# Attention in a three-branch mixer: the product with the values put on token partitions, its division moved behind it, one turn back for four tiles

## The chip, the cores and the metric

The kernel runs on one core of a Trainium2 chip. The metric is the device time of one execution in microseconds (us), as the median of several runs. Five engines work side by side, each through its own list of instructions in a fixed order: PE (matrix products), DVE (vector work), ACT (activations), POOL (general work) and SP (transfers).

## The reference

Two layers, each with three sub-layers: a gated feed-forward step, a mixer, and another feed-forward step, over 512 tokens and 1024 channels in float32. The mixer adds three branches; the one that is changed is attention with a forget bias, 8 heads of 64 channels:

```python
def block(args):                      # 128 queries at a time
    qi, Fi, pi = args
    s = jnp.einsum('bhqd,bhkd->bhqk', qi, k) * scale
    s = s + (Fi[..., :, None] - F[..., None, :])
    s = jnp.where(kpos[None, :] <= pi[:, None], s, -jnp.inf)
    p = jax.nn.softmax(s, axis=-1)
    return jnp.einsum('bhqk,bhkd->bhqd', p, v)
...
o_a = _fox_attention(q, k, v, fl, f_bias) @ wpa
o_b = _rg_lru_branch(...) @ wpb
o_c = _rwkv7_branch(...) @ wpc
```

## The kernel before

Activations stay channels-on-partitions between the steps: `aout[:, p, :]` holds the 128 channels of two heads (a pair) for all 512 tokens. `mix_branches` issues three things interleaved: the attention (`fox`, four pairs per layer), then the linear recurrence (`lru`), and beside both the steps of the RWKV branch, the gate products, and background work on the next layer's conditioning vectors. The `yield` values in `fox_pair` are the costs by which the other two streams are advanced (lines 1140 to 1152). The framework's scheduler then sets every engine's order from its own estimate of durations, so an edit in the attention also moves the instructions around it. Each engine then runs its list strictly in order.

In `fox_pair`, each pair takes four query tiles `i` of 128 tokens, and for each of the two heads `hh`: two products give the scores `sc` (lines 1054, 1055); DVE adds the bias and takes the maximum (1058, and 1062 for the earlier keys); DVE negates the maximum (1066); ACT takes the exponential in place in `e` and its sum `rs` (1068); DVE inverts the sum (1069) and multiplies the whole row block by it (1070). Then PE turns `e` in 128x128 pieces (1077), ACT or DVE copies the turned block to `et` (1080, 1082), and PE multiplies with the values:

```python
mm(out=po[64 * hh : 64 * hh + 64, 0:P], lhsT=vs[:, j, hh * 64 : hh * 64 + 64],
   rhs=et[:, j * P : (j + 1) * P], start=j == 0, stop=j == i, skip_group_check=True)
```

The 64 value columns of a head are the weights and the 128 queries stream through, so the output lies channels-on-partitions, the two heads on the two halves. ACT copies it to `aout` (1091). Each such product in float32 is two instructions on PE in the trace. Per pair there are 20 products, so 160 over both layers and 320 instructions. Lines 201 to 203 are the large projections' products (512 columns), lines 194 and 196 split weights into a rounded part and a rest (the rest on POOL inside the mixer), lines 866 and 868 are an inverse of RWKV on DVE, and line 913 is an RWKV product with full weights and 64 columns.

Of the kernel before, what the change touches and what calls it, by code (L numbers as in the profile page):

```python
# [9 lines left out]
F32 = mybir.dt.float32  # L10
F32R = mybir.dt.float32r
AF = mybir.ActivationFunctionType
ALU = mybir.AluOpType
PSUM = bass.MemoryType.PSUM

P = 128
# [3 lines left out]
NT = S // P  # L20
# [9 lines left out]
DH = 64  # L30
# [29 lines left out]
class Trunk:  # L60
# [952 lines left out]
    def fox_pair(self, l, p, ap):  # L1013


        nc = self.nc
        mm = nc.tensor.matmul


        qs = ap.tile([P, 2, S], F32R, tag="q", bufs=1, name=self.nm("q"))  # L1020
        ks = ap.tile([P, 2, S], F32R, tag="k", bufs=1, name=self.nm("k"))
        kl = self.kl
        vs = ap.tile([P, NT, P], F32, tag="v", bufs=1, name=self.nm("v"))
        ps = self.gemm("aq", p)
        for hh, r in enumerate(ROWS):
            nc.scalar.activation(qs[r, hh, :], ps[r], AF.Copy)
            nc.vector.tensor_tensor(out=qs[ROWS[1 - hh], hh, :], in0=ps[r], in1=qs[r, hh, :].bitcast(F32), op=ALU.subtract)
        yield 5.2
        ps = self.gemm("ak", p)
        for hh, r in enumerate(ROWS):  # L1030
            nc.scalar.activation(ks[r, hh, :], ps[r], AF.Copy)
            nc.vector.tensor_tensor(out=kl[r, hh, :], in0=ps[r], in1=ks[r, hh, :].bitcast(F32), op=ALU.subtract)
            nc.gpsimd.tensor_copy(ks[ROWS[1 - hh], hh, :], ks[r, hh, :])
        yield 5.2
        vf = ap.tile([P, S], F32, tag="e", bufs=2, name=self.nm("vf"))
        nc.vector.tensor_copy(vf, self.gemm("av", p))
        pv = self.ps("s")
        for t in range(NT):
            nc.tensor.transpose(pv[:, t * P : (t + 1) * P], vf[:, t * P : (t + 1) * P], self.ident)
        nc.scalar.activation(vs.rearrange("p t c -> p (t c)"), pv, AF.Copy)  # L1040
        yield 5.2
        fbs = []
        for hh in range(2):
            fbs.append(ap.tile([P, S], F32, tag="fb", bufs=2, name=self.nm("fb")))
            nc.sync.dma_start(out=fbs[hh], in_=self.nF[2 * p + hh : 2 * p + hh + 1, :].broadcast_to([P, S]))
        yield 0.9
        for i in range(NT):
            n = i * P
            es = []
            for hh, fb in enumerate(fbs):  # L1050
                fm = ap.tile([P, P], F32, tag="fm", bufs=2, name=self.nm("fm"))
                nc.gpsimd.tensor_tensor(out=fm, in0=fb[:, n : n + P], in1=self.causal, op=ALU.add)
                sc = self.ps("s")
                mm(out=sc[:, 0 : n + P], lhsT=qs[:, hh, n : n + P], rhs=ks[:, hh, 0 : n + P], start=True, stop=False)
                mm(out=sc[:, 0 : n + P], lhsT=qs[:, hh, n : n + P], rhs=kl[:, hh, 0 : n + P], start=False, stop=True)
                e = ap.tile([P, S], F32, tag="e", bufs=2, name=self.nm("e"))
                m = self.sp.tile([P, 2], F32, tag="mx", name=self.nm("mx"))
                nc.vector.tensor_tensor_reduce(out=e[:, n : n + P], in0=sc[:, n : n + P], in1=fm, scale=0.125,
                                               scalar=-3e38, op0=ALU.add, op1=ALU.max, accum_out=m[:, 0:1])
                last = m[:, 0:1]  # L1060
                if i:
                    nc.vector.tensor_tensor_reduce(out=e[:, 0:n], in0=sc[:, 0:n], in1=fb[:, 0:n], scale=0.125,
                                                   scalar=last, op0=ALU.add, op1=ALU.max, accum_out=m[:, 1:2])
                    last = m[:, 1:2]
                nm = self.sp.tile([P, 1], F32, tag="nmx", name=self.nm("nmx"))
                nc.vector.tensor_scalar(out=nm, in0=last, scalar1=-1.0, scalar2=None, op0=ALU.mult)
                rs = self.sp.tile([P, 1], F32, tag="rsum", name=self.nm("rsum"))
                nc.scalar.activation(e[:, 0 : n + P], e[:, 0 : n + P], AF.Exp, bias=nm, accum_out=rs)
                nc.vector.reciprocal(rs, rs)
                nc.vector.tensor_scalar(out=e[:, 0 : n + P], in0=e[:, 0 : n + P], scalar1=rs, scalar2=None, op0=ALU.mult)  # L1070
                es.append(e)
                yield 0.2 * (i + 1)
            ets = []
            for hh, e in enumerate(es):
                pt = self.ps("s")
                for j in range(i + 1):
                    nc.tensor.transpose(pt[:, j * P : (j + 1) * P], e[:, j * P : (j + 1) * P], self.ident)
                et = ap.tile([P, S], F32, tag="et", bufs=2, name=self.nm("et"))
                if hh:
                    nc.scalar.activation(et[:, 0 : n + P], pt[:, 0 : n + P], AF.Copy)  # L1080
                else:
                    nc.vector.tensor_copy(et[:, 0 : n + P], pt[:, 0 : n + P])
                ets.append(et)
                yield 0.1 * (i + 1)

            po = self.ps("s")
            for j in range(i + 1):
                for hh, et in enumerate(ets):
                    mm(out=po[64 * hh : 64 * hh + 64, 0:P], lhsT=vs[:, j, hh * 64 : hh * 64 + 64],  # L1089
                       rhs=et[:, j * P : (j + 1) * P], start=j == 0, stop=j == i, skip_group_check=True)  # L1090
            nc.scalar.activation(self.aout[:, p, n : n + P], po[:, 0:P], AF.Copy)
            yield 0.25 * (i + 1)

    def mix_branches(self, l):

# [405 lines left out]
```

## Time and profile before

| what | value |
|---|---|
| runs | 3092.88, 3094.02, 3103.51 us; median 3094.02 |
| profiled execution | 3098.59 us, its span 3096.5 us |
| PE busy | 2931.2 us, 95% of the span |
| DVE busy | 1880.0 us, 61% |
| attention stretches | 496 to 786 us and 2028 to 2318 us of the span |
| mean granted clock of PE | 0.983 |

The busy time of PE counts overlapping products once, and its ends are modelled, so 95% means that PE is rarely without a product in flight. The numbers behind an arrow in the waits name the instruction that ended the wait. `PEld` is the load of weights, which runs beside products.

### The profile page before, as it was taken

The page shows a single profiled execution, that of the slowest core. Times are in us where ns is not written, and L with a number is a line of the kernel's source. Part 1 is how long each engine was busy: PE and PEld are TensorE (multiplying, and loading weights), DVE is VectorE, ACT ScalarE, POOL GpSimd, SP SyncE. Part 2 cuts the span into 40 slices and gives each one's busy share as a digit, 9 for nine tenths or more (in the row PEclk, how much of TensorE's full clock was granted, in tenths as well). Part 3 has the DMA queues.
Part 4 walks back from the last instruction along what each step waited for, and adds up shares of the span by engine and source line. Part 5 has one row for each costly group of instructions (what it writes and reads, how often), then busy time and mean ns, then how long its engine had stood idle before and what let it go on. Part 6 is the DMA issues. An engine that isn't in the chain of part 4 may idle for free. (4 is left out here: it accounts for less than half of the span.)

```text
span 3096.5 us, 39351 instructions
## 1 busy us (share of the span) xinstructions
PE 2931.2 (95%) x15330; PEld 2338.4 (76%) x15330; DVE 1880.0 (61%) x3534; ACT 1142.2 (37%) x1699; POOL 554.8 (18%) x379
## 2 busy tenths in 40 slices
PE   7999998998989998999999999889989899999998
PEld 5888886676766788888888887767666677788887
DVE  6755567666785656565656546667676756654435
ACT  4322253332545635222342214433335554342212
POOL 0000142333232013000130002423333320230000
PEclk9999999999999999999999999999999999999999
DMA  8634333333342463434434424433333424632221
GB/s 280 224 109 146 115 117 101 88 87 102 94 113 67 139 203 118 139 122 143 129 117 136 133 92 145 127 99 93 88 90 93 107 73 143 204 116 96 89 68 62
DMA packets 389402, 372.17 MB, mean 120 GB/s; under 512 B 54964, under 2 KB 318544, under 8 KB 389216
## 3 DMA queue, kind: packets, MB, share of 16 engines
q1 hardware_dynamic: 377048, 350.14, 37.0%
q10 hardware_dynamic: 12168, 19.53, 1.7%
q8 instruction: 120, 1.97, 0.3%
q14 instruction: 66, 0.54, 0.1%
HBM read 347.54 MB, written 22.09 MB: 119 GB/s over the span
## 5 line engine op out<-in xcount | busy, mean ns | idle before, releaser
L194 ACT ACTIVATE hi<-raw 128x1024 fp32r<-128x1024 f32 (+1 forms) x460 | 469.2, 1028 | 1248.9 <-PE pg L202 501.3
L196 POOL TENSOR_TENSOR lo<-raw,hi 128x1024 fp32r<-128x1024 f32 x164 | 408.0, 2490 | 1692.1 <-ACT hi L194 1639.2
L201 PE MATMUL pg<-hhi,hi 128*128 128x512 f32 (+1 forms) x1744 | 680.4, 393 | 13.7 <-DVE ks L645 3.7
L202 PE MATMUL pg<-hlo,hi 128*128 128x512 f32 (+1 forms) x1744 | 673.5, 389 | 2.9 <-DVE nm L343 2.9
L203 PE MATMUL pg<-hhi,lo 128*128 128x512 f32 (+1 forms) x1744 | 674.8, 391 | 0.0
L196 DVE TENSOR_TENSOR lo<-raw,hi 128x1024 fp32r<-128x1024 f32 (+1 forms) x296 | 342.5, 1165 | 301.3 <-ACT hi L194 296.1
L201 PEld LDWEIGHTS pg<-hhi,hi 128*128 128x128 f32 x1744 | 330.9, 190 | 86.9 <-issue 10.5
L203 PEld LDWEIGHTS pg<-hhi,lo 128*128 128x128 f32 x1744 | 330.6, 190 | 66.5 <-issue 2.1
L202 PEld LDWEIGHTS pg<-hlo,hi 128*128 128x128 f32 x1744 | 331.2, 190 | 65.3 <-issue 4.7
L202 PE MATMUL pr<-hlo,hi 128*128 128x512 f32 (+1 forms) x816 | 300.4, 368 | 5.1 <-DVE nm L343 2.9
L201 PE MATMUL pr<-hhi,hi 128*128 128x512 f32 (+1 forms) x816 | 301.5, 370 | 2.2 <-ACT hhi L397 2.2
L203 PE MATMUL pr<-hhi,lo 128*128 128x512 f32 (+1 forms) x816 | 300.7, 369 | 0.0
L284 DVE SCALAR_TENSOR_TENSOR acc<-raw,cact,acc 128x512 f32<-128x512 f32 x224 | 187.7, 838 | 48.7 <-DMA raw<-in_ada_w_dram 44.3
L202 PEld LDWEIGHTS pr<-hlo,hi 128*128 128x128 f32 x816 | 155.0, 190 | 34.2 <-issue 7.4
L201 PEld LDWEIGHTS pr<-hhi,hi 128*128 128x128 f32 x816 | 155.1, 190 | 28.1 <-ACT hhi L397 2.6
L203 PEld LDWEIGHTS pr<-hhi,lo 128*128 128x128 f32 x816 | 155.2, 190 | 27.4
L352 POOL TENSOR_TENSOR rstd<-var,mhalf 128x1 f32<-128x1 f32 x48 | 30.2, 630 | 470.5 <-DVE var L351 461.9
L201 PE MATMUL ps<-hi,ahi 128*128 128x512 f32 x264 | 103.5, 392 | 0.0
L203 PE MATMUL ps<-hi,alo 128*128 128x512 f32 x264 | 103.3, 391 | 0.0
L202 PE MATMUL ps<-lo,ahi 128*128 128x512 f32 x264 | 103.1, 391 | 0.0
L480 DVE TENSOR_TENSOR su<-pg,su 128x512 f32<-128x512 f32 x42 | 28.9, 689 | 115.2 <-PE pg L203 115.1
L480 DVE TENSOR_TENSOR su<-pr,su 128x512 f32<-128x512 f32 x42 | 29.0, 690 | 110.0 <-PE pr L203 105.9
(443 smaller groups left out, 4956.9 us busy)
## 6 DMA issues: line engine op xcount, KB each, us to landing
raw<-in_ffn_up_dram SPq DMA_DIRECT2D x70, 1024.0 KB
raw<-in_w_in_dram SPq DMA_DIRECT2D x132, 512.0 KB
raw<-in_ada_w_dram SPq DMA_DIRECT2D x64, 1024.0 KB
raw<-in_ffn_down_dram SPq DMA_DIRECT2D x40, 1024.0 KB
raw<-in_ffn_up_dram SPq DMA_DIRECT2D x36, 512.0 KB
gspill<-gate ACTq DMA_DIRECT2D x48, 256.0 KB
gate<-gspill SPq DMA_DIRECT2D x48, 256.0 KB
ada<-in_ada_w_dram SPq DMA_DIRECT2D x16, 512.0 KB
```

The source lines that it names most:

```text
L194: self.nc.scalar.activation(hi, v, AF.Copy)
L196: eng.tensor_tensor(out=lo, in0=v, in1=hi.bitcast(F32), op=ALU.subtract)
L201: mm(out=ps, lhsT=lhi, rhs=rhi, start=start, stop=False, **kw)
L202: mm(out=ps, lhsT=lhi, rhs=rlo, start=False, stop=False, **kw)
L203: return mm(out=ps, lhsT=llo, rhs=rhi, start=False, stop=stop, **kw).ins
L284: nc.vector.scalar_tensor_tensor(out=acc, in0=r[:, i, :], scalar=c, in1=acc, op0=ALU.mult, op1=ALU.add)
L352: nc.gpsimd.tensor_tensor(out=r, in0=v, in1=self.mhalf, op=ALU.pow)
L480: nc.vector.tensor_tensor(out=su, in0=pss[1], in1=su, op=ALU.mult)
```

## The change

The weights and the stream of the product with the values change places: the turned block `et` (128 keys by 128 queries) is the weight, and the head's 64 value columns stream. The output lies tokens-on-partitions, both heads side by side in 128 columns. The multiplication of `e` by the inverse sum is left out; the inverse is taken once for both heads (two columns of `rs`), and DVE multiplies the output by it as it moves it from PSUM to the new tile `ao`. After the four query tiles of a pair, PE turns `ao` in four 128x128 pieces into one PSUM bank, and ACT copies all 512 columns to `aout` at once.

```diff
--- before.py
+++ after.py
@@ -1044,9 +1044,11 @@
             fbs.append(ap.tile([P, S], F32, tag="fb", bufs=2, name=self.nm("fb")))
             nc.sync.dma_start(out=fbs[hh], in_=self.nF[2 * p + hh : 2 * p + hh + 1, :].broadcast_to([P, S]))
         yield 0.9
+        ao = ap.tile([P, NT, P], F32, tag="ao", bufs=1, name=self.nm("ao"))
         for i in range(NT):
             n = i * P
             es = []
+            rs = self.sp.tile([P, 2], F32, tag="rsum", name=self.nm("rsum"))
             for hh, fb in enumerate(fbs):
                 fm = ap.tile([P, P], F32, tag="fm", bufs=2, name=self.nm("fm"))
                 nc.gpsimd.tensor_tensor(out=fm, in0=fb[:, n : n + P], in1=self.causal, op=ALU.add)
@@ -1064,12 +1066,10 @@
                     last = m[:, 1:2]
                 nm = self.sp.tile([P, 1], F32, tag="nmx", name=self.nm("nmx"))
                 nc.vector.tensor_scalar(out=nm, in0=last, scalar1=-1.0, scalar2=None, op0=ALU.mult)
-                rs = self.sp.tile([P, 1], F32, tag="rsum", name=self.nm("rsum"))
-                nc.scalar.activation(e[:, 0 : n + P], e[:, 0 : n + P], AF.Exp, bias=nm, accum_out=rs)
-                nc.vector.reciprocal(rs, rs)
-                nc.vector.tensor_scalar(out=e[:, 0 : n + P], in0=e[:, 0 : n + P], scalar1=rs, scalar2=None, op0=ALU.mult)
+                nc.scalar.activation(e[:, 0 : n + P], e[:, 0 : n + P], AF.Exp, bias=nm, accum_out=rs[:, hh : hh + 1])
                 es.append(e)
                 yield 0.2 * (i + 1)
+            nc.vector.reciprocal(rs, rs)
             ets = []
             for hh, e in enumerate(es):
                 pt = self.ps("s")
@@ -1084,12 +1084,17 @@
                 yield 0.1 * (i + 1)
 
             po = self.ps("s")
-            for j in range(i + 1):
-                for hh, et in enumerate(ets):
-                    mm(out=po[64 * hh : 64 * hh + 64, 0:P], lhsT=vs[:, j, hh * 64 : hh * 64 + 64],
-                       rhs=et[:, j * P : (j + 1) * P], start=j == 0, stop=j == i, skip_group_check=True)
-            nc.scalar.activation(self.aout[:, p, n : n + P], po[:, 0:P], AF.Copy)
+            for hh, et in enumerate(ets):
+                for j in range(i + 1):
+                    mm(out=po[:, 64 * hh : 64 * hh + 64], lhsT=et[:, j * P : (j + 1) * P],
+                       rhs=vs[:, j, hh * 64 : hh * 64 + 64], start=j == 0, stop=j == i, skip_group_check=True)
+            nc.vector.tensor_tensor(out=ao[:, i, :].rearrange("p (h d) -> p h d", h=2), in0=po[:, 0:P].rearrange("p (h d) -> p h d", h=2),
+                                    in1=rs.unsqueeze(2).to_broadcast([P, 2, DH]), op=ALU.mult)
             yield 0.25 * (i + 1)
+        pt = self.ps("s")
+        for i in range(NT):
+            nc.tensor.transpose(pt[:, i * P : (i + 1) * P], ao[:, i, :], self.ident)
+        nc.scalar.activation(self.aout[:, p, :], pt, AF.Copy)
 
     def mix_branches(self, l):
 
```

Outside the two mixers, every engine's order is the same as before; inside them the scheduler orders anew, alike in both layers. Three places follow.

PE, first pair, from the scores of the third query tile's second head to the first head's turns. Before:

```order
L1054 MATMUL ps_4082<-k_3576,q_3575 128x384
L1055 MATMUL ps_4082<-kl_3494,q_3575 128x384
L202 MATMUL pg_4270<-hlo,hi_4274 128x512
L203 MATMUL pg_4270<-hhi,lo_4275 128x512
L201 MATMUL pg_4270<-hhi,hi_4274 128x512
L202 MATMUL pg_4270<-hlo,hi_4274 128x512
L203 MATMUL pg_4270<-hhi,lo_4275 128x512
L201 MATMUL pg_4270<-hhi,hi_4274 128x512
L202 MATMUL pg_4270<-hlo,hi_4274 128x512
L203 MATMUL pg_4270<-hhi,lo_4275 128x512
L201 MATMUL pg_4270<-hhi,hi_4274 128x512
L1077 MATMUL ps_4095<-ident,e_4049 128x128 x3
```

With the change (scores are lines 1056 and 1057 there):

```order
L1056 MATMUL ps_4073<-k_3576,q_3575 128x384
L1057 MATMUL ps_4073<-kl_3494,q_3575 128x384
L203 MATMUL pg_4261<-hhi,lo_4266 128x512
L201 MATMUL pg_4261<-hhi,hi_4265 128x512
L202 MATMUL pg_4261<-hlo,hi_4265 128x512
L203 MATMUL pg_4261<-hhi,lo_4266 128x512
L201 MATMUL pg_4261<-hhi,hi_4265 128x512
L202 MATMUL pg_4261<-hlo,hi_4265 128x512
L1077 MATMUL ps_4084<-ident,e_4043 128x128 x3
```

Nine large products stood between these scores and the turns, now six. Over both layers, 856 products of 512 columns stand between scores and their turns before, and 736 with the change (and 540 and 452 others).

PE, the end of the first pair. Before:

```order
L1089 MATMUL ps_4257<-et_4238,v_3577 64x128
L1089 MATMUL ps_4257<-et_4231,v_3577 64x128
L1089 MATMUL ps_4257<-et_4238,v_3577 64x128
L1089 MATMUL ps_4257<-et_4231,v_3577 64x128
L1089 MATMUL ps_4257<-et_4238,v_3577 64x128
L1089 MATMUL ps_4257<-et_4231,v_3577 64x128
L1089 MATMUL ps_4257<-et_4238,v_3577 64x128
L202 MATMUL pg_4354<-hlo,hi_4355 128x512
L203 MATMUL pg_4354<-hhi,lo_4356 128x512
```

With the change (line 1096 is the turn of `ao`):

```order
L1077 MATMUL ps_4218<-ident,e_4203 128x128 x4
L203 MATMUL pg_4261<-hhi,lo_4266 128x512
L1089 MATMUL ps_4242<-v_3577,et_4216 128x64 x4
L1089 MATMUL ps_4242<-v_3577,et_4223 128x64 x4
L1096 MATMUL ps_4252<-ident,ao_3938 128x128 x3
L201 MATMUL pg_4261<-hhi,hi_4265 128x512
L1096 MATMUL ps_4252<-ident,ao_3938 128x128
L202 MATMUL pg_4261<-hlo,hi_4265 128x512
```

The product stands as two runs of four, one for each head, and the turns of `ao` follow it at once, the last one behind one large product. In all, the product's instructions stand in 66 runs before and in 68 with the change.

DVE, first pair, third and fourth query tile. Before:

```order
L1058 ISA e_4085,mx_4086<-ps_4082,fm_4080 128x128
L1058 ISA mx_4086 128x1
L1066 TENSOR_SCALAR nmx_4053<-mx_4050 128x1
L1062 ISA e_4085,mx_4086<-ps_4082,fb_3935,mx_4086 128x256
L1062 ISA mx_4086 128x1
L1066 TENSOR_SCALAR nmx_4089<-mx_4086 128x1
L1069 RECIPROCAL rsum_4055<-rsum_4055 128x1
L1070 TENSOR_SCALAR e_4049<-e_4049,rsum_4055 128x384
L1069 RECIPROCAL rsum_4091<-rsum_4091 128x1
L1070 TENSOR_SCALAR e_4085<-e_4085,rsum_4091 128x384
L1082 COPY et_4099<-ps_4095 128x384
```

With the change (1060, 1064, 1068 are the lines 1058, 1062, 1066 of before; 1072 is the inverse, 1091 the multiplication of the output):

```order
L1060 ISA e_4076,mx_4077<-ps_4073,fm_4071 128x128
L1060 ISA mx_4077 128x1
L1064 ISA e_4076,mx_4077<-ps_4073,fb_3935,mx_4077 128x256
L1064 ISA mx_4077 128x1
L1068 TENSOR_SCALAR nmx_4080<-mx_4077 128x1
L1082 COPY et_4088<-ps_4084 128x384
L1072 RECIPROCAL rsum_4037<-rsum_4037 128x2
L1091 TENSOR_TENSOR ao_3938<-ps_4116,rsum_4037 128x128
L1060 ISA e_4130,mx_4131<-ps_4127,fm_4125 128x128
L1060 ISA mx_4131 128x1
```

The two pairs of inverse and multiplication in front of the copy `et` are gone; behind the copy stand one inverse and the multiplication of the output, which waits for PE, and behind it the next tile's scores.

## Rows read from the trace of the kernel before

**Rows 1.** The page of before, part 1: busy us (share) xinstructions

```profile
PE 2931.2 (95%) x15330; PEld 2338.4 (76%) x15330; DVE 1880.0 (61%) x3534; ACT 1142.2 (37%) x1699; POOL 554.8 (18%) x379
```

**Rows 2.** The attention stretches: length, busy us by engine (instructions), clock

```profile
496.00:786.00 290.00, 263.13 (x1634) 196.51 (x1635) 194.68 (x541) 99.08 (x205) 89.45 (x74) 0.97 0.34 94
2028.00:2318.00 290.00, 264.77 (x1647) 197.89 (x1648) 196.95 (x563) 100.25 (x207) 88.89 (x74) 0.98 0.35 95
```

**Rows 3.** Waits, 496 to 786: who, whom: us in total, times, longest

```profile
PE ps L1077 <- DVE e L1070: 14.2, 9, 2.8
```

**Rows 4.** The same waits, 2028 to 2318

```profile
PE ps L1077 <- DVE e L1070: 11.3, 8, 2.8
```

**Rows 5.** Groups by line: xcount | busy us, mean ns | idle before

```profile
L1070 DVE TENSOR_SCALAR e<-e,rsum 128x128 f32<-128x128 f32 (+3 forms) x64 | 39.9, 624 | 0.9
L1069 DVE RECIPROCAL rsum<-rsum 128x1 f32<-128x1 f32 x64 | 10.0, 156 | 6.5 <-ACT e L1068 5.6
L1058 DVE CUSTOM_DVE_ANT_0 e<-ps,fm 128x128 f32<-128x128 f32 x64 | 18.5, 289 | 41.2 <-PE ps L1055 40.1 <-issue 0.7
L1091 ACT ACTIVATE aout<-ps 128x128 f32<-128x128 f32 x32 | 8.9, 277 | 42.0 <-PE ps L1089 42.0
L1089 PE MATMUL ps<-et,v 128*64 128x128 f32 x320 | 37.8, 294 | 2.0 <-DVE T L866 2.0
```

**Rows 6.** Line L1070: ns min/median/max, first and last start, forms

```profile
L1070 DVE TENSOR_SCALAR e<-e,rsum x64: 270/414/2376, 507.9 to 2307.5; 128x128 f32<-128x128 f32 x16, 128x256 f32<-128x256 f32 x16, 128x384 f32<-128x384 f32 x16, 128x512 f32<-128x512 f32 x16
```

**Rows 7.** Timeline, pair 3 of the second layer: start, length, engine, line

```profile
2297.61 2.37 POOL L196 TENSOR_TENSOR lo<-raw,hi 128x1024 fp32r<-128x1024 f32 x1 [1.48 <-ACT hi L194]
2297.94 0.18 ACT L1068 ACTIVATION_READ_ACCUMULATOR e<-e,nmx 128x1 f32 x1
2298.36 1.83 DVE L1070 TENSOR_SCALAR e<-e,rsum 128x384 f32<-128x384 f32 x1
2300.34 0.52 PE L1077 MATMUL ps<-ident,e 128*128 128x128 f32 x3 [1.56 <-DVE e L1070]
```

**Rows 8.** Timeline, pair 0 of the first layer, the same chain

```profile
528.44 0.19 ACT L1068 ACTIVATION_READ_ACCUMULATOR e<-e,nmx 128x1 f32 x1
528.66 0.16 DVE L1069 RECIPROCAL rsum<-rsum 128x1 f32<-128x1 f32 x1
528.86 0.49 DVE L1070 TENSOR_SCALAR e<-e,rsum 128x512 f32<-128x512 f32 x1
```

**Rows 9.** Timeline of TensorE, two runs of the product L1089

```profile
524.29 0.49 PE L1077 MATMUL ps<-ident,e 128*128 128x128 f32 x3
524.71 0.43 PE L1089 MATMUL ps<-et,v 128*64 128x128 f32 x2
525.08 0.50 PE L1054 MATMUL ps<-k,q 128*128 128x512 f32 x1
525.74 0.87 PE L1089 MATMUL ps<-et,v 128*64 128x128 f32 x10
526.54 0.50 PE L1054 MATMUL ps<-k,q 128*128 128x512 f32 x1
```

**Rows 10.** Timeline of TensorE: products of 64 columns, and four turns

```profile
545.77 0.40 PE L201 MATMUL pg<-hhi,hi 128*128 128x512 f32 x1
546.01 0.39 PE L202 MATMUL pg<-hlo,hi 128*128 128x512 f32 x1
546.24 0.55 PE L913 MATMUL pc<-S,AR 128*128 128x64 f32 x4
546.73 0.45 PE L916 MATMUL pc<-UV,AM 128*64 128x64 f32 x4
...
2308.43 0.60 PE L1077 MATMUL ps<-ident,e 128*128 128x128 f32 x4
2308.87 0.60 PE L808 MATMUL pr<-ident,KB 128*128 128x128 f32 x4
```

**Rows 11.** The chain that ended last, 2028 to 2318, by line

```profile
by line: PE pg L203 10.2%; PE pg L201 10.1%; PE pg L202 9.2%; DVE Y L868 5.6%; PE ps L1089 4.6%; DVE e L1070 3.6%; PE ps L1077 3.0%; DVE acc L284 3.0%; DVE T L866 2.8%; issue 2.8%; PE pr L822 2.6%; PE pr L844 2.4%; PE ps L1054 2.1%; PE pc L
```

## The prediction

> **What bounds the kernel now.** I read part 1 of the page first, then the table of stretches, then the waits, then the chain, and last the timeline around one wait. Part 1 of the page shows PE busy for 95% of the span and DVE for 61% [rows 1]: a gain must shorten PE's own list or the times in which it stands still. The change touches only the two attention stretches, 580 us in all. There PE is busy 263.1 and 264.8 of 290 us [rows 2], so it stands still 26.9 and 25.2 us, 52.1 together. The waits say for whom: the turns of the exponentials (L1077) wait for DVE's multiplication by the inverse sum (L1070), 14.2 us in 9 waits and 11.3 us in 8 [rows 3, 4]. That is 25.5 us in 17 waits, half of the idle time, and 1.5 us each. In the second stretch, the chain that ended last holds L1070 for 3.6% of 290 us, 10.4 us [rows 11], so these are not waits beside the path.
>
> Two pieces of timeline show what such a wait consists of. In the short case the sum is ready at 528.63, the inverse starts at 528.66 and the multiplication ends at 529.35: 0.72 us from the exponential to the turn [rows 8]. In the long case the exponential is done at 2298.12, but a weight split on POOL began at 2297.61; the multiplication starts at 2298.36, takes 1.83 us instead of some 0.4 and ends with POOL's instruction, 2.07 us after the exponential, and PE waits 1.56 us [rows 7]. The line's median is 414 ns, its longest 2376 and its mean 624 [rows 5, 6]: (624 - 414) x 64 = 13.4 us of its 39.9 are such stretches.
>
> **The change part by part.** The sum is made on the profiled execution, 3098.6 us (span 3096.5 and 2.1 around it), which lies 4.6 above the median of the runs; its difference is then taken from the median, 3094.0.
>
> *PE's list.* Before, the product is 320 instructions in 66 runs. A run of two takes 0.37 us from its start to the next product's start, a run of ten 0.80 [rows 9]: 0.054 for each instruction and 0.26 for a run. The two heads lie on two halves of the array; a turn's 128 columns take 0.11 us [rows 10], twice as long, so the halves work at the same time. Entering costs besides: three turns before the run take 0.42 us [rows 9] where four take 0.44 [rows 10], so 0.09 a run. Together 320 x 0.054 + 66 x (0.26 + 0.09) = 40.4 us. After, the form is full weights and 64 columns, as in L913: four take 0.49 us up to a run on half the array [rows 10], 0.12 each with the entry of that run, 0.10 without. I take 0.11, so 35.2 us (32 to 38.4), in 68 runs that need no entry. The 32 added turns cost 0.11 each [rows 10], 3.5 us. After: 38.7, that is -1.7 against 40.4 (from -5 to +1.5); with some turns in runs of their own I take -1.
>
> [...]
>
> *The wait of the turns.* 64 inverses and 64 multiplications leave the chain between exponential and turn, so each turn may start 0.72 us earlier where DVE is idle and about 2.07 where POOL holds it [rows 7, 8]. But the turns also stand earlier in PE's list: 856 large products covered the 64 chains, now 736, and 540 others are now 452. At 0.24 us from one large product to the next and 0.1 for the small ones [rows 10] that is 120 x 0.24 + 88 x 0.1 = 38 us less cover, 0.59 for each chain. So a chain gains 0.13 us in the short case and 1.5 in the long one. Over 17 waits that is 2.2 to 25.5 us. The waits average 1.5 us and the stretched multiplications account for most of the long ones; I take two thirds, -17. What is late next is the exponential on ACT, which waits for DVE's maxima.
>
> *DVE and ACT.* DVE loses 39.9 and 10.0 us [rows 5], and gains 32 inverses of 0.156 (5.0) and 32 multiplications out of PSUM. No such operation stands in the rows; the nearest is L1058, 128 columns out of PSUM with a second operand, 0.289 [rows 5], so 9.2 (the inverse's 0.156 and twice 0.289 bound it: 5 to 18.5). That leaves -35.7 of 391.6 us in the two stretches, 9%. PE's other idle time there, 52.1 - 25.5 = 26.6 us, is largely for DVE; a tenth of it goes, -2 (0 to -8). ACT loses 32 copies, 8.9 us, and gains 8 of four times the columns, at most 8.9: nothing, and no engine waits for ACT here beyond the turn's chain.
>
> *The new wait.* The four turns of `ao` follow the pair's last product. The first three need query tiles that are long done; the last needs DVE's multiplication of the fourth. From the product's end that takes 0.29 us and two handovers of some 0.15 (0.15 us pass between the end of L1070 and the turn [rows 7]), 0.6; three turns and a large product hide 0.56. Eight pair ends cost nothing if DVE is free, and up to 2 us each if DVE is as far behind as in the long case; behind the waiting turn stands all of PE's list. I take 0.5 each, +4 (0 to 16). The multiplication also waits on DVE for the product where ACT did before: 42.0 us in 32 copies [rows 5]. Behind it on DVE stand the next tile's maxima, whose scores PE issues after the product anyway, so most of this wait stands where DVE would have waited.
>
> *Clock.* [...]
>
> Sum: -1 - 17 - 2 + 4 - 3 = -19, so 3079.6 by the profiled execution and **3075 us** by the median.
>
> **The rivals.**
>
> *The cover is given back.* The scheduler moves the turns up by as much as the chain became shorter, so the waits stay, with other instructions in front. For it speaks that 0.59 of the 0.72 us are given back in the short case; against it that the stretched multiplications were in no plan. The 17 waits then give 3 us, the clock nothing: -1 - 3 - 1 + 4 = -1, 3093 us.
>
> [...] If entry and end cost come with any small product and not with the half array, the change saves only 320 x 0.054 = 17.3 us of the old form and pays 35.2: +18, +3.5 for the turns, and -17 - 2 + 4 - 3 as above, so +3.5 and 3098 us. [...] Against it: the large product in front of L913 keeps its step (546.01 to 546.24, as 545.77 to 546.01 [rows 10]), while the turns in front of a packed run take 0.09 longer [rows 9].
>
> *DVE's queue blocks (slower).* The output's multiplication stands on DVE in strict order and waits for PE, 42.0 us in all if ACT's waits move there as they are [rows 5]. On ACT nothing hung on it; on DVE the RWKV inverse and the next maxima do. If two thirds reach PE as idle time, that is +28, against -1 - 10 - 0 + 8 for the rest, as the shorter chain also gains less behind a blocked queue: +25, 3119 us. It decides once DVE's waits at that line exceed about the 35.7 us that DVE saves. Against it: in the list, scores that are issued after the product stand right behind the multiplication on DVE.
>
> **How the numbers follow.** My forecast 0.58, its own range 3060 to 3086; the cover given back 0.19, about 3093; the packing 0.10, about 3098; DVE's queue 0.13, 3100 to 3125. About 0.5% (15.5 us) is what a measurement of this kernel can tell from no change, so "faster" means below 3078.5. Of the forecast 0.46 lies below it and 0.12 within; the first rival is no change (0.19); of the packing 0.08 is no change and 0.02 slower; of DVE's queue 0.10 is slower than 3109.5 and 0.03 not. Faster 0.46, same 0.42, slower 0.12. The range that leaves out 2 in 10 is 3060 to 3099.
>
> **What would show it.** The waits of L1077 should name ACT's exponential, with 5 to 12 us in place of 25.5. The product's runs should step by 0.10 to 0.12 us with no longer step before them; steps of 0.05 or of 0.2 would prove that term wrong. DVE's busy time in the stretches should fall by about 36 us. The turns of `ao` should wait under 1 us each; waits of 2 us, or DVE idle at line 1091 for over 35 us, would make the prediction wrong, and so would idle time of PE in the stretches that stays near 52 us.

## The result, and the profile after

The changed kernel takes 3126.94 us (median of four runs, 3125.61 to 3133.77) against 3094.6 for the kernel before beside it: a ratio of 1.0103, 95% interval 1.0079 to 1.0128. It is slower by 1%, 32 us; the forecast was 3075. Its profiled span is 3123.6 us, 27.1 more than before.

In the page of the changed kernel, part 1 gives busy time, share of the span and instructions of each engine, as [rows 1] do for before:

```profile
PE 2949.6 (94%) x15362; PEld 2366.3 (76%) x15362; DVE 1871.7 (60%) x3470; ACT 1138.3 (36%) x1675; POOL 555.4 (18%) x379
```

DVE lost 64 instructions but only 8.3 us of busy time. The waits that the forecast set out to shorten did shorten. These are the waits of PE in its two attention stretches after, 496 to 786 us and then 2044 to 2334 us (total us, times, longest), which answer to [rows 3, 4]:

```profile
PE ps L1077 <- ACT e L1069: 5.5, 5, 2.2
PE ps L1089 <- DVE et L1082: 4.3, 2, 3.9
...
PE ps L1096 <- DVE ao L1091: 0.4, 1, 0.4
```

```profile
PE ps L1077 <- ACT e L1069: 7.0, 4, 3.4
PE ps L1089 <- DVE et L1082: 4.4, 2, 3.9
...
PE ps L1096 <- DVE ao L1091: 0.5, 1, 0.5
```

The turns (L1077) now wait for ACT's exponential, 12.5 us in 9 waits where it was 25.5 in 17. New is a wait of 3.9 us in each layer for the copy `et` (L1082); it is followed up below. The groups by line after (xcount | busy us, mean ns | idle before), which answer to [rows 5]:

```profile
L1089 PE MATMUL ps<-v,et 128*128 128x64 f32 x320 | 48.4, 284 | 8.7 <-DVE et L1082 8.7
...
L1096 PE MATMUL ps<-ident,ao 128*128 128x128 f32 x32 | 8.5, 318 | 0.9 <-DVE ao L1091 0.9
...
L1091 DVE TENSOR_TENSOR ao<-ps,rsum 128x128 f32<-128x128 f32 x32 | 9.2, 288 | 20.7 <-PE ps L1089 20.4
...
L1072 DVE RECIPROCAL rsum<-rsum 128x2 f32<-128x2 f32 x32 | 5.0, 157 | 2.8 <-ACT e L1069 2.8
```

And a run of the product on TensorE's timeline (start, length), which answers to [rows 9, 10]:

```profile
684.97 0.88 PE L1089 MATMUL ps<-v,et 128*128 128x64 f32 x6
685.69 0.39 PE L1096 MATMUL ps<-ident,ao 128*128 128x128 f32 x2
685.91 0.33 PE L1089 MATMUL ps<-v,et 128*128 128x64 f32 x2
```

Six products from 684.97 to 685.69 are 0.12 us each, two turns from there to 685.91 are 0.11 each, as costed.

Where then did the time go? The table of stretches of the changed kernel (length, then busy us and instructions of PE, PEld, DVE, ACT, POOL, then the granted clock) has the attention stretches, which answer to [rows 2], and behind each the rest of its mixer:

```profile
496.00:786.00 290.00, 267.91 (x1659) 208.79 (x1658) 184.63 (x541) 97.25 (x194) 89.13 (x74) 0.96 0.34 94
2044.00:2334.00 290.00, 265.69 (x1638) 208.04 (x1639) 180.65 (x513) 96.04 (x189) 89.47 (x74) 0.95 0.33 93
...
786.00:1126.00 340.00, 312.88 (x1651) 236.04 (x1650) 215.38 (x370) 165.14 (x239) 75.02 (x36) 0.95 0.34 99
2334.00:2602.00 268.00, 243.88 (x1384) 181.54 (x1382) 180.48 (x343) 143.11 (x211) 73.35 (x35) 0.96 0.30 84
```

The same rest of the mixers in the kernel before:

```profile
786.00:1110.00 324.00, 304.34 (x1662) 231.41 (x1662) 211.32 (x405) 165.99 (x240) 74.82 (x36) 0.98 0.37 105
2318.00:2575.00 257.00, 236.94 (x1364) 176.82 (x1362) 171.46 (x331) 144.37 (x210) 74.78 (x36) 0.97 0.32 87
```

The two rests grew from 581 to 608 us for about the same products (3026 instructions on PE before, 3035 after). With the attention stretches taken as equally long, all 27 us of the loss stand there, where the diff touches nothing; everything outside the two mixers takes 1935.5 us before and 1935.6 after. PE's idle time in the rests (length less PE's busy time) grew from 39.7 to 51.2 us, and the time lost to the lower clock (length times one minus the granted clock, summed from the unrounded clock records) from 12.6 to 27.4. In the attention stretches the idle time fell from 52.1 to 46.4 us, but the clock's loss rose from 15.3 to 23.8.

How a new wait of PE comes about is seen in three places. The first is the wait for `et`, which uses up within the attention much of what the turns gained there. This is the timeline of the changed kernel near the end of the first layer's attention (start us, us, engine, line, output<-inputs, idle before and who ended it):

```profile
767.33 0.69 DVE L794 TENSOR_TENSOR rout<-vs,pr 128x512 f32<-128x512 f32 x1 [0.25 <-PE pr L792]
...
767.54 2.40 POOL L196 TENSOR_TENSOR lo<-raw,hi 128x1024 fp32r<-128x1024 f32 x1 [11.73 <-ACT hi L194]
...
767.93 2.04 DVE L866 TENSOR_TENSOR T<-Y 64x28 f32<-64x28 f32 x1
...
770.22 0.19 DVE L866 TENSOR_TENSOR T<-Y 64x39 f32<-64x39 f32 x1
770.35 2.37 POOL L196 TENSOR_TENSOR lo<-raw,hi 128x1024 fp32r<-128x1024 f32 x1 [0.42 <-ACT hi L194]
...
770.45 2.33 DVE L868 TENSOR_TENSOR Y<-Y,T 64x39 f32<-64x39 f32 x1
...
773.05 0.20 DVE L868 TENSOR_TENSOR Y<-Y,T 64x48 f32<-64x48 f32 x1
...
775.00 0.67 DVE L1082 COPY et<-ps 128x512 f32<-128x512 f32 x1
...
775.73 1.54 PE L1089 MATMUL ps<-v,et 128*128 128x64 f32 x6 [3.92 <-DVE et L1082]
```

L866 and L868 are steps of RWKV's inverse; a wider one (64x48) takes 0.20 us. Those that start while POOL makes a weight split take 2.04 and 2.33 us and end within 0.06 us of POOL's instruction. Behind them in DVE's list stands the copy `et`, and behind that PE, for 3.92 us. So a stretch like that of the removed L1070 [rows 7] stands here on another DVE step. The second place is 27 us later, already in the rest of the mixer:

```profile
794.62 2.37 POOL L196 TENSOR_TENSOR lo<-raw,hi 128x1024 fp32r<-128x1024 f32 x1 [5.29 <-DMA raw<-in_ada_w_dram]
795.00 2.27 DVE L1253 TENSOR_SCALAR ge<-ge 128x512 f32<-128x512 f32 x1 [0.82 <-ACT ge L1252]
...
798.76 1.54 PE L844 MATMUL pr<-T,AM 64*64 64x64 f32 x24 [2.92 <-DVE T L881]
```

The third is the largest new wait. In the rest of each mixer, PE's waits after the change are headed by the first of these lines; both stand in the two layers alike, and in the kernel before L333 ends no wait of PE, and the wait at L844 is 1.0 and 1.5 us:

```profile
PE pg L201 <- DVE rst L333: 4.8, 1, 4.8
...
PE pr L844 <- DVE T L881: 2.9, 1, 2.9
```

The timeline of the first layer shows two held steps in front of it:

```profile
857.65 2.40 POOL L196 TENSOR_TENSOR lo<-raw,hi 128x1024 fp32r<-128x1024 f32 x1
...
857.75 2.85 DVE L957 TENSOR_TENSOR Yt<-Yt,gsum 128x512 f32<-128x512 f32 x1
...
862.60 2.36 POOL L196 TENSOR_TENSOR lo<-raw,hi 128x1024 fp32r<-128x1024 f32 x1 [2.55 <-ACT hi L194]
...
862.64 2.35 DVE L330 TENSOR_SCALAR rsq<-rst 128x8 int32<-128x8 int32 x1
...
868.36 0.76 PE L201 MATMUL pg<-hhi,hi 128*128 128x512 f32 x1 [4.79 <-DVE rst L333]
```

L957 and L330 are steps of one chain, the normalisation of RWKV's output. Unheld they take 0.69 and 0.17 us, so the two holds are 4.3 us, nearly all of the wait. Behind them in DVE's list stand the rest of this chain and a convolution of the recurrence (L1240), and PE goes on when these are through.

The granted clock about and behind these waits is lower than the span's mean of 0.978, 0.91 and 0.63 for the first two:

```profile
766.00:776.00 10.00, 6.08 (x36) 4.93 (x35) 9.37 (x21) 3.87 (x7) 4.77 (x2) 0.91 0.48 143
...
796.00:810.00 14.00, 11.24 (x113) 8.64 (x115) 8.30 (x11) 4.04 (x6) 2.65 (x2) 0.63 0.29 76
```

In the 14 us about and behind the second wait the granted clock is 0.63: the clock's records of both kernels hold two levels, 1.0 and 0.5, so that is about three quarters of the time at the lower one (10.2 of 14 us). Those of the changed kernel have the lower level for 6.8 us from 774.3, for 10.2 us from 798.1 and for 6.8 us from 866.4, and in the kernel before not once between 775 and 890 us. The second and third wait are 2.9 and 4.8 us, and half of the time at the lower level behind their ends is 4.8 and 2.4, together 14.9 us. The first layer's rest is 16 us longer (324 to 340). Other waits come and go there, so this compares sizes and is not a full account.

I counted every DVE instruction that took over 0.4 us longer than the short instances (the shortest eighth) of its line and shape. Before there are 111 with 166 us of excess, after 110 with 171. L1070's 15.6 us are gone, L868's fell from 26 to 8 and L284's from 20 to 8; L866 went from 11 to 24, L1253 (L1248 before) to 14, L333 from 6 to 13, L957 from nothing to 9. The stretches were not removed; they came down elsewhere.

### The profile page after: what moved, and what is told of

The parts are those of the page before. It is cut to its first block, busy times and chain, and to the rows that moved or that the text cites. A ratio compares the mean times of both kernels' runs of the same rounds, so it can differ in the third digit from the quotient of the medians.

```text
span 3123.6 us, 39377 instructions
## 1 busy us (share of the span) xinstructions
PE 2949.6 (94%) x15362; PEld 2366.3 (76%) x15362; DVE 1871.7 (60%) x3470; ACT 1138.3 (36%) x1675; POOL 555.4 (18%) x379
## 5 line engine op out<-in xcount | busy, mean ns | idle before, releaser
L284 DVE SCALAR_TENSOR_TENSOR acc<-raw,cact,acc 128x512 f32<-128x512 f32 x224 | 175.6, 784 | 45.6 <-DMA raw<-in_ada_w_dram 41.2
L203 PEld LDWEIGHTS pr<-hhi,lo 128*128 128x128 f32 x816 | 155.1, 190 | 27.4
L480 DVE TENSOR_TENSOR su<-pg,su 128x512 f32<-128x512 f32 x42 | 29.0, 690 | 118.4 <-PE pg L203 118.4
L480 DVE TENSOR_TENSOR su<-pr,su 128x512 f32<-128x512 f32 x42 | 29.0, 690 | 112.6 <-PE pr L203 112.6
```

The lines of the kernel that those rows point to most:

```text
L203: return mm(out=ps, lhsT=llo, rhs=rhi, start=False, stop=stop, **kw).ins
L284: nc.vector.scalar_tensor_tensor(out=acc, in0=r[:, i, :], scalar=c, in1=acc, op0=ALU.mult, op1=ALU.add)
L480: nc.vector.tensor_tensor(out=su, in0=pss[1], in1=su, op=ALU.mult)
```

## The experiments

Three theories went in. One: POOL's weight splits hold whichever DVE step comes under them, and the change only moved which. Two: any move of the order around the mixers' schedule costs about so much. Three: the new orientation of the product costs the time. (A fourth, that DVE waits at L1091 for the product, had its 20.4 us in 12 waits above, under its limit of 35.7.)

**e1: new orientation, old division.** The inverse and the multiplication go back onto the exponentials, and ACT copies `ao`:

```diff
+                nc.vector.reciprocal(rs[:, hh : hh + 1], rs[:, hh : hh + 1])
+                nc.vector.tensor_scalar(out=e[:, 0 : n + P], in0=e[:, 0 : n + P], scalar1=rs[:, hh : hh + 1], scalar2=None, op0=ALU.mult)
...
-            nc.vector.tensor_tensor(out=ao[:, i, :]..., in0=po[:, 0:P]..., in1=rs..., op=ALU.mult)
+            nc.scalar.activation(ao[:, i, :], po[:, 0:P], AF.Copy)
```

> The changed kernel with one part undone: the tokens stay on the partitions and the final turns stay, but the division is again made by DVE on the exponentials (a reciprocal and a multiplication for each of the two heads), and ACT copies the product out. Theory 1 (the time went into DVE steps that now meet POOL's weight splits, because the stretched division on the exponentials no longer takes them): the division is back as a target of the splits, some 8 us of stretch a mixer return to it, the steps L866/L868 and L1253 lose theirs, and the time is 3090 to 3108 us. Theory 3 (the new orientation of the product itself costs the time): nothing of the loss goes, 3118 to 3135 us. Theory 2 (any move of the order around the mixer's schedule costs about so much): no place is foretold, anything from 3090 to 3135 us; its test is the placebos.

Measured: 3086.97 us, ratio 0.997 (0.9959 to 0.9982), a little better than theory one's range. The new form of the product alone isn't what costs: theory three falls. The excess of stretched steps is 144 us, with 8.6 of it on the division and L868 at 12.6.

**e2: the kernel before without the division.**

```diff
-                nc.vector.reciprocal(rs, rs)
-                nc.vector.tensor_scalar(out=e[:, 0 : n + P], in0=e[:, 0 : n + P], scalar1=rs, scalar2=None, op0=ALU.mult)
```

> The kernel before with the division by the sum left out (reciprocal and multiplication on the exponentials are not made, so the output is not divided by the sum). It takes 39.9 + 10.0 us of DVE's work away and adds nothing. Theory 1: the splits on POOL that stretched the division stretch other DVE steps instead, the excess over the short form stays at about 61 us a mixer, DVE's busy time falls by less than 40 us, and the time is 3095 to 3125 us, no better than before although work is gone. Theory 3 (the orientation costs): this kernel has none of it, and gains what the waits of the turns held, 3070 to 3085 us. Theory 2: 3080 to 3125 us.

Measured: 3105.54 us, ratio 1.0029 (1.0017 to 1.0041). Some 50 us of DVE's work are gone and nothing was added, yet the time is no better. DVE's busy time fell by 31.7 us (1880.0 to 1848.3), the excess is 157 us, and L1246 (the step that is L1253 after) has 14.4 of it. Theories one and two both allow it.

**e3 and e4: the mixers' splits on DVE,** in the kernel before and in the changed one:

```diff
-        self.wide, self.on_pool = False, True
+        self.wide, self.on_pool = False, False
```

> The kernel before with the weight splits of the mixers made by DVE instead of POOL. POOL is nearly idle in the mixers, so no DVE step is stretched beyond its short form (61 us of excess a mixer go), while DVE gets some 40 splits a mixer of about 0.55 us, 22 us. Theory 1: DVE's busy time falls by 60 to 80 us in all, and the time is 3060 to 3090 us. If the stretched steps are not what PE waits for: 3090 to 3110 us, DVE's queue being no shorter where it matters. Theory 2 says only that the order moves, and that the time does within 35 us.

> The changed kernel with the same move of the mixers' weight splits from POOL to DVE. Theory 1: with no stretched step left, the loss goes: the time lies 8 us below to 8 us above the kernel before with the same move, and the stretches with the low clock shrink from 140 us to about 105 us. Theory 3 (orientation): the gap of some 30 us between the two stays. Theory 2 (the order alone): the gap is of any size, either sign, within 35 us.

Measured: 2995.80 us, ratio 0.9676 (0.9653 to 0.9699), and 2987.35, ratio 0.9647 (0.9627 to 0.9667). Both gain far more than foretold, 99 and 140 us, and the changed kernel is now the faster one, by 8.5 us, half a microsecond outside theory one's range: all runs of e4 (2985.58 to 2988.20) lie below all of e3 (2993.93 to 2996.64). This although a mixer has 64 splits of 1.22 us on DVE and not the 40 of 0.55 us of the expectation. The excess is 31 and 36 us. One part of the expectation failed: DVE's busy time did not fall by 60 to 80 us, it rose by 4.1 in e3 (1880.0 to 1884.1). The gain is not a shorter list of DVE; it is PE's idle time (165.3 to 97.2 us) and the clock's loss (51.5 to 19.9).

**e5 and e6: each split on POOL in two halves.**

```diff
+        if self.on_pool and k % 2 == 0:
+            for a in (0, k // 2):
+                c2 = slice(a, a + k // 2)
+                self.nc.gpsimd.tensor_tensor(out=lo[:, c2], in0=v[:, c2], in1=hi[:, c2].bitcast(F32), op=ALU.subtract)
+            return hi, lo
```

> The kernel before with each weight split of POOL made as two instructions of half the length (about 1.2 us each in place of 2.4 us), on POOL as before. The sum of POOL's work is the same or a little more. Theory 1 (a DVE step that comes under a split is held until that instruction ends): the longest DVE steps shrink from 2.4 us to about 1.4 us, more of them are hit, the excess stays between 100 and 190 us in the whole run, and since PE's waits come from single long steps the time is 3070 to 3095 us. A rival on the gain without splits on POOL, that the second half of a weight simply came late from POOL: splitting it in two makes it no earlier, 3090 to 3105 us, and the longest steps are as before.

> The changed kernel with the same halving of POOL's weight splits. Theory 1: it gains more than the kernel before does, as it lost more to single long steps, and lands at 3080 to 3110 us; the wait of 3.9 us behind L866 and L868 and that behind L1253 fall to under 2 us each. If the late weight or the orientation is the cause: 3115 to 3135 us.

Measured: 3078.91 us, ratio 0.9949 (0.993 to 0.9968), and 3098.53, ratio 1.0018 (1.0006 to 1.0031): 15 and 28 us less, both in theory one's ranges. The longest L868 (L873 there) fell from 2331 ns to 1302. In both layers of e6 the wait for `et` fell from 3.92 us to 0.55 and the one behind L1253 from 2.92 to 1.85, both under 2 us as foretold; the one that L333 ends fell from 4.8 to 3.6. The length of one POOL instruction matters, at no less work on POOL (its busy time rose from 555 to 597 and 600 us). The two times alone would prove little, as e7 shows what another order can do.

**e7 and e8: one pacing number moved,** in before and in the changed kernel, with no instruction added or removed:

```diff
-FOX_COST, LRU_COST = 24.5, 11.9
+FOX_COST, LRU_COST = 24.0, 11.9
```

> The kernel before with one number of the mixer's pacing moved (FOX_COST 24.5 to 24.0): the same instructions, interleaved a little otherwise from the mixers on. Theory 1 with theory 2 (the order only decides which DVE steps meet POOL's splits): the time moves by 5 to 30 us, more likely up, 3085 to 3125 us, with the excess of the stretched steps between 140 and 185 us. If the order hardly matters: 3090 to 3100 us.

> The changed kernel with the same move of the pacing (FOX_COST 24.0). Theories 1 and 2: the time moves by 5 to 30 us, as likely down as up, 3095 to 3140 us, so that the gap to the kernel before with the same move differs from 32 us by more than 10 us. Theory 3 (the orientation costs by itself): the gap stays at 25 to 40 us.

Measured: 3142.49 us, ratio 1.0164 (1.0141 to 1.0188), and 3135.26, ratio 1.0138 (1.0118 to 1.0159). The kernel before loses 49 us, more than foretold and more than the change cost, and the gap of 32 us between the kernels turns into 7 the other way. So the size and sign of the loss belong to the order, not to the edit: theory two holds too.

**e9 and e10: the pacing moved with the mixers' splits on DVE.** Both edits above.

> The kernel before with both: the mixers' weight splits on DVE and the pacing number at 24.0. With the splits on POOL the same number cost 49 us (3142 against 3094). Theory 1 (the order matters because it decides which DVE steps meet POOL's splits): with the splits gone the number costs little, 2985 to 3008 us, that is within 12 us of the 2996 us at 24.5. If the order matters by itself (theory 2 without theory 1): 3025 to 3055 us.

> The changed kernel with both. Theory 1: within 12 us of the 2987 us at 24.5, 2976 to 2999 us, and below the kernel before with both by 3 to 15 us, the change's own gain. Theory 2 without theory 1: any place from 2980 to 3030 us.

Measured: 3005.18 us, ratio 0.9721 (0.9701 to 0.9741), and 2998.88, ratio 0.9698 (0.968 to 0.9716), in theory one's ranges. The same number that cost 49 us in the kernel before now costs 9, and 12 in the changed kernel. The order matters mainly through the splits on POOL. But 9 and 12 us are also more than the 8.5 and 6.3 us by which the changed kernel is ahead in these two pairs, so that gain is not clear of the order.

**e11 and e12: what is left of the change.** With the mixers' splits on DVE, the division on ACT (e11), and the division back on the exponentials (e12, as e1):

```diff
-            nc.vector.tensor_tensor(out=ao[:, i, :]..., in0=po[:, 0:P]..., in1=rs..., op=ALU.mult)
+            for hh in range(2):
+                nc.scalar.activation(ao[:, i, 64 * hh : 64 * hh + 64], po[:, 64 * hh : 64 * hh + 64], AF.Copy, scale=rs[:, hh : hh + 1])
```

> The changed kernel with the mixers' weight splits on DVE, and the division on the product made by ACT (two copies of 64 columns with the reciprocal as scale, for each token tile) instead of one DVE multiplication. DVE loses 32 steps of 0.29 us, 9 us, and their waits for PE at the head of its queue; ACT gets 64 copies of some 0.2 to 0.3 us in place of 32. If DVE's wait for the product at L1091 (theory 4) costs: 2970 to 2984 us; if not, 2984 to 2995 us.

> The kernel with the new orientation but the division still on the exponentials, with the mixers' weight splits on DVE. It lies between the two kernels without splits on POOL (2996 and 2987 us). If the gain of 8.5 us is the division's move: 2993 to 3000 us; if it is the orientation's (the packed matmuls): 2983 to 2990 us.

Measured: 2991.93 us (2991.12 to 2993.07) and 2991.47 (2987.24 to 2993.22). No gain is seen from taking DVE's wait at L1091 away. e12 falls between its two ranges: which half of the change gives the 8.5 us stays open.

**e13: the same POOL work, with nobody waiting for it.** Moving the splits also shortens them (median 2.40 us on POOL, 1.22 on DVE), so each weight's rest can be ready earlier, and e4 alone can't say which of the two counted. In e13 the mixers' splits are on DVE, and POOL makes each subtraction once more into a tile that nobody reads:

```diff
+        if self.spare:
+            sp = self.sp.tile([P, k, c], F32R, tag="spare", bufs=1, name=self.nm("spare"))
+            self.nc.gpsimd.tensor_tensor(out=sp, in0=v, in1=hi.bitcast(F32), op=ALU.subtract)
```

> The changed kernel with the mixers' weight splits on DVE, and beside each of them the same subtraction on POOL into a spare tile that nobody reads. Theory 1 (a DVE step that comes under a long POOL instruction is held): the stretched DVE steps return, some 60 us of excess a mixer, and the time is 3060 to 3150 us. If the late halves of the weights cost the time: 2980 to 3005 us, as without splits on POOL.

Measured: 3168.99 us, ratio 1.0244 (1.0223 to 1.0265): 182 us above e4, beyond theory one's range on its side. DVE pays twice here, as its own splits are stretched too (44 us of an excess of 211). Two waits for the spare tile reach PE's weight loads, 8.5 us in all, and three reach ACT, 6.8 us, through buffers that the idle work holds; DVE never waits for it. PE's waits that DVE ended (those over 0.15 us) sum to 113.8 us before the change, 109.5 after it, 27.3 in e4 and 126.0 in e13; those that ACT ended to 46.4 in e4 and 73.9 in e13. The line of L868 (L871 in e13) by duration in ns, minimum, median and maximum: in the kernel before, in e4, and in e13:

```profile
L868 DVE TENSOR_TENSOR Y<-Y,T x120: 166/208/2402, 497.6 to 2453.9; 64x15 f32<-64x15 f32 x16, 64x28 f32<-64x28 f32 x16, 64x39 f32<-64x39 f32 x16, 64x48 f32<-64x48 f32 x16
```

```profile
L868 DVE TENSOR_TENSOR Y<-Y,T x120: 152/199/464, 492.8 to 2361.9; 64x15 f32<-64x15 f32 x16, 64x28 f32<-64x28 f32 x16, 64x39 f32<-64x39 f32 x16, 64x48 f32<-64x48 f32 x16
```

```profile
L871 DVE TENSOR_TENSOR Y<-Y,T x120: 145/201/2399, 508.9 to 2535.0; 64x15 f32<-64x15 f32 x16, 64x28 f32<-64x28 f32 x16, 64x39 f32<-64x39 f32 x16, 64x48 f32<-64x48 f32 x16
```

The longest is 2.4 us with long POOL instructions beside it, whoever uses their result, and 0.46 without. Minimum and median hardly move. L1253 shows the same, in the changed kernel and in e4:

```profile
L1253 DVE TENSOR_SCALAR ge<-ge x16: 399/1353/2271, 795.0 to 2591.9; 128x512 f32<-128x512 f32 x16
```

```profile
L1253 DVE TENSOR_SCALAR ge<-ge x16: 400/420/428, 762.2 to 2452.9; 128x512 f32<-128x512 f32 x16
```

**e14: no weight split on POOL at all,** in the changed kernel, with the edit of e4 and this one:

```diff
-                self.on_pool = c == 0 and not begin
+                self.on_pool = False
```

> The changed kernel with the weight splits outside the mixers moved from POOL to DVE too (36 instructions of 2.62 us). Theory 1: DVE's steps beside them are no longer stretched (L416, L650: some 20 us of excess in all), but PE waits little there: 2970 to 2987 us. If DVE's queue is the tighter one there: 2987 to 3000 us.

Measured: 2981.21 us (2977.11 to 2982.31), ratio 0.9632 (0.961 to 0.9653): the fastest here, 3.7% below the kernel before and 4.7% below the changed one.

The spans of all these follow one sum. PE's idle time is the span less its busy time, the clock's loss is the span times one minus the mean granted clock (unrounded; the column has three places), and what is left is about PE's work at full clock:

| kernel | span | PE busy | clock | idle | clock's loss | left |
|---|---|---|---|---|---|---|
| before | 3096.5 | 2931.2 | 0.983 | 165.3 | 51.5 | 2879.7 |
| changed | 3123.6 | 2949.6 | 0.978 | 174.0 | 68.7 | 2880.9 |
| e7 | 3136.2 | 2942.3 | 0.978 | 193.9 | 67.9 | 2874.5 |
| e13 | 3171.4 | 2959.4 | 0.974 | 212.0 | 83.9 | 2875.4 |
| e3 | 2992.1 | 2894.9 | 0.993 | 97.2 | 19.9 | 2875.0 |
| e4 | 2986.0 | 2898.3 | 0.992 | 87.7 | 23.1 | 2875.3 |

What is left differs by 6 us over all six; the spans differ by 185. Up to these 6 us, waits and the time at the lower clock are what these kernels differ in.

## Why the prediction was wrong, step by step

- *PE's list* (-1): held. The steps are the 0.11 to 0.12 us that were costed, and the last column above moves by 1 us. The rival at 3098 us, the packing's, falls.
- *The wait of the turns* (-17): -13 there. The row for the long case has the multiplication end 0.21 us after POOL's instruction and not with it, which changes little. But the prediction took the stretched multiplications for a property of L1070, which would go with it. They were a property of POOL's list: L868's longest is 2399 ns beside the idle POOL work of e13 and 464 in e4, without splits on POOL in the mixers. This is the step that failed: L1070's 15.6 us of stretches went, but other DVE steps started under the splits and were stretched (166 us in all before, 171 after), and the question was who waits for those. For L866 and L868 it is `et` and PE, 3.9 us in each layer; for L957 and L330 it is the large products, 4.8 us in each layer.
- *DVE and ACT* (-2): the -35.7 us of busy time came out as -26.3 in the stretches (391.6 to 365.3) and -8.3 in the whole run. The work went, but the stretches grew from 166 to 171 us instead of falling by L1070's part. PE's other idle time in the attention did not fall by 2: it rose from 26.6 to 33.9 us, 8.7 of them the wait for `et`.
- *The new wait* (+4): 0.9 us in 2 waits. Too careful, and "DVE's queue blocks", the rival on the slow side, had the right sign for another reason: its waits at L1091 stayed at 20.4 us, and taking them off DVE (e11) gained nothing.
- *Clock* (-3): +8.5 in the attention (15.3 to 23.8) and +17.2 in the whole run (51.5 to 68.7), the largest single part of the 27.1 us. The prediction let the clock only gain. No run shows its term of -3, a fifth of the clock's loss going with PE's idle time: in the attention the idle time fell by 5.7 us (52.1 to 46.4) and the loss rose. The row about and behind the second wait, at 0.63, shows the clock beside a new wait of 2.9 us in another place.
- "The change touches only the two attention stretches" was true of the diff and false of the time: all 27 us stand in the rest of the mixers. No term, and no rival, stood for a changed order there.

Against its own kernel, the change is worth this (median after less median before), by what stands beside it: +32.3 us with the splits on POOL, +19.6 with halved splits, -7.2 with the other pacing number, -8.5 with the mixers' splits on DVE, -6.3 with that and the other pacing. The prediction's -19, with a range from -34 to +5, left out the first two. That the splits on POOL cause the stretches and most of what the order costs is shown (e3, e4, e9, e10, e13). That the 32 us of this one order are made of the waits named above and the clock behind them is read from the trace, and e6 agrees, in which these waits are shorter; why this order brings just these steps under a split stays open.

## What to carry to other kernels

Where one engine's long instructions hold another's, a stretched instruction need not be a cost of its own line (here 15.6 us of stretches left with L1070, and the sum went from 166 to 171): before costing its removal as a gain, look at what else can start under the same hold and who waits for it. Move the holder first (here 3.2% for one word), and measure the edit then. Where a scheduler sets the order, move one neutral number once (here 1.6%) to learn how much any edit can win or lose by chance.

## What the runs showed that was not expected

Which DVE steps a split held differs by line, and at one line by who started first. Of the DVE steps that start under a split on POOL with over 0.6 us of it to go, in the changed kernel, L1253 was held 10 times of 10, L866 12 of 12, L650 18 of 18, L957 4 of 4, and before the change L1070 10 of 10; all of them read and write SBUF alone. Steps with an operand from PSUM were never held: L1060 0 of 5, L645 0 of 16, L480 0 of 7, the new L1091 0 of 2, and of 25 copies none. Nor were two steps of one or two columns that read SBUF, L1068 0 of 9 and L1072 0 of 4, nor before the change two of 512 columns that read one tile in SBUF, L890 and L954, 0 of 2 each. At L330, of SBUF alone, it went by the order: in six of its eight meetings with a split it began between 0.11 us before the split and 0.01 us after its start and took 0.17 us; in the two in which it began 0.04 us after the split, one of them at 862.64 us above, it took 2.35. It has 128x8 elements, so a small step was held too. What it is in the operands that decides is not shown. The new multiplication on the output wasn't held in the two meetings there are, where the old one was in all ten: the change took the right step away, and what it uncovered was not in view.
